# A row-sum kernel on one core: loads of contiguous 8 MB blocks, and sums stored block by block from ScalarE's queue

## The chip, the cores and the metric

The kernel runs on one NeuronCore of a Trainium2 chip. The metric is device time in microseconds (us); lower is better. Runs of one kernel on one chip agree to about 0.3%, so differences of 0.1 to 0.2% need several rounds, and most statements below about such differences rest on five. In the profiles DVE is VectorE, ACT is ScalarE, SP is SyncE; "SPq" and "ACTq" are the queues from which these two issue transfers. A transfer is carried out by 16 DMA engines as a list of descriptors, each of which moves one contiguous piece.

## The reference

```python
# x: (32, 512, 1024) float32
def reference(x):
    return np.sum(x, axis=-1).astype(np.float32)
```

The input is 16384 rows of 4 KB, 64 MB (67.1 million bytes) in all; the output is one float per row, 64 KB. Every byte is read once and added once, so this is a streaming problem.

## The kernel before

Partition `p` of 128 owns rows `128*p` to `128*p+127`. A tile is 16 rows of every partition (8 MB), three tiles are buffered, and VectorE and ScalarE sum eight rows each. One load is thus 128 pieces of 64 KB that lie 512 KB apart in memory. The last of the eight tiles is loaded in ever smaller pieces, so that little work is left after the last landing. One store of 64 KB ends the kernel.

```python
    C = R // P                                   # 128 rows per partition
    x_p = x_flat.rearrange("(p c) d -> p (c d)", p=P)
    out2d = out.rearrange("a (b c) -> (a b) c", c=C)
    G = 16                                       # rows per partition in a tile
    T = C // G                                   # 8 tiles
    xpool = ctx.enter_context(tc.tile_pool(name="x", bufs=3))
    ...
    def load(xt, c0, a, b):
        nc.sync.dma_start(out=xt[:, a:b], in_=x_p[:, c0 * D + a : c0 * D + b])
    ...
    for t in range(T - 1):
        c0 = t * G
        xt = xpool.tile([P, G * D], F32, tag="xt", name="xt")
        load(xt, c0, 0, G * D)
        rows_dve(xt, c0, 0, G // 2)              # one reduction of 8 rows
        rows_act(xt, c0, G // 2, G // 2)         # eight activations with a sum
    ...                                          # last tile: pieces of 8, 4, 2, 1 rows, then
    cuts = [j * D + k for k in (0, D // 2, 3 * D // 4, D)]      # the last row in three pieces
    ...
    acc = [part[:, 0:1], part[:, 1:2], res[:, C - 1 : C]]
    for i, (a, b) in enumerate(zip(cuts, cuts[1:])):
        pairs_dve(xt, a, b, acc[i - 1] if i else 0.0, acc[i])   # each step starts from the sum before
    nc.sync.dma_start(out=out2d, in_=res)
```

Of the kernel before, what the change touches and what calls it, by code (L numbers as in the profile page):

```python
# [1 line left out]

# [4 lines left out]

F32 = mybir.dt.float32
ADD = mybir.AluOpType.add


@with_exitstack
def kernel(
    ctx: ExitStack,
    tc: tile.TileContext,
    x: bass.AP,
    out: bass.AP,
):
    nc = tc.nc
    P = nc.NUM_PARTITIONS  # L20

    x_flat = x.flatten_outer_dims()
    R, D = x_flat.shape
    assert R % P == 0
    C = R // P

    x_p = x_flat.rearrange("(p c) d -> p (c d)", p=P)
    out2d = out.rearrange("a (b c) -> (a b) c", c=C)

    G = 16  # L30
    assert C % G == 0
    T = C // G

    xpool = ctx.enter_context(tc.tile_pool(name="x", bufs=3))
    rpool = ctx.enter_context(tc.tile_pool(name="res", bufs=1))
    res = rpool.tile([P, C], F32, name="res")
    part = rpool.tile([P, 4], F32, name="part")

    def load(xt, c0, a, b):
        nc.sync.dma_start(out=xt[:, a:b], in_=x_p[:, c0 * D + a : c0 * D + b])  # L40

    def rows_dve(xt, c0, j, n):
        nc.vector.tensor_reduce(  # L43
            out=res[:, c0 + j : c0 + j + n],
            in_=xt[:, j * D : (j + n) * D].rearrange("p (j d) -> p j d", d=D),
            axis=mybir.AxisListType.X,
            op=ADD,
        )

    def rows_act(xt, c0, j, n):  # L50
        for i in range(j, j + n):
            v = xt[:, i * D : (i + 1) * D]
            nc.scalar.activation(  # L53
                out=v,
                in_=v,
                func=mybir.ActivationFunctionType.Copy,
                accum_out=res[:, c0 + i : c0 + i + 1],
            )

    def pairs_dve(xt, a, b, first, acc):  # L60
        h = (b - a) // 2
        nc.vector.tensor_tensor_reduce(  # L62
            out=xt[:, a : a + h],
            in0=xt[:, a : a + h],
            in1=xt[:, a + h : b],
            scale=1.0,
            scalar=first,
            op0=ADD,
            op1=ADD,
            accum_out=acc,  # L70
# [5 lines that stand above are left out]
        load(xt, c0, 0, G * D)  # L76
        rows_dve(xt, c0, 0, G // 2)
        rows_act(xt, c0, G // 2, G // 2)

    c0 = (T - 1) * G  # L80
    xt = xpool.tile([P, G * D], F32, tag="xt", name="xt")
    j = 0
    runs = []
    for n in (8, 4, 2, 1):
        load(xt, c0, j * D, (j + n) * D)
        runs.append((j, n))
        j += n
    cuts = [j * D + k for k in (0, D // 2, 3 * D // 4, D)]
    for a, b in zip(cuts, cuts[1:]):
        load(xt, c0, a, b)  # L90

    for j, n in runs:
        if n > 1:
            rows_dve(xt, c0, j, n // 2)
            rows_act(xt, c0, j + n // 2, n // 2)
        else:
            rows_act(xt, c0, j, 1)
    acc = [part[:, 0:1], part[:, 1:2], res[:, C - 1 : C]]
    for i, (a, b) in enumerate(zip(cuts, cuts[1:])):
        pairs_dve(xt, a, b, acc[i - 1] if i else 0.0, acc[i])  # L100

    nc.sync.dma_start(out=out2d, in_=res)


# [1 line left out]
_INS = ['x']  # L106
_OUTS = [((32, 512), 'float32')]


# [23 lines left out]
```

## Time and profile before

| what | before |
|---|---|
| median of the runs | 163.95 us |
| span of the profiled run | 162.4 us |
| busy: DMA (loads' queue) / DVE / ACT | 96.3% / 43% / 43% |
| one 8 MB tile: load / DVE / ACT | 19.3 to 19.7 us / 8.69 us / 8.4 us |

From the page of the kernel before: busy time of two engines, the moved GB/s in 40 equal slices of the span, the DMA queues (packets, MB, share of 16 engines), and the chain of work that ended last (followed back from the last instruction, at each step to what released it), by engine and by line.

```profile
DVE 69.9 (43%) x16; ACT 69.0 (43%) x129; POOL 0.2 (0%) x4
...
GB/s 258 517 323 452 517 355 420 517 371 404 501 355 436 517 371 404 517 371 404 517 452 325 517 468 307 517 468 323 501 484 323 484 484 307 452 420 408 418 350 20
...
q1 hardware_dynamic: 2160, 67.18, 96.3%
...
DMA 85%; DVE 11%; SPq 1%; issue 1%; DVEq 0%
```

The loads fill the span and the two computing engines are idle more than half of it. A single slice above 500 GB/s is only the way in which whole 64 KB descriptors are booked into 4 us slices; the mean (414 GB/s over the span) is what counts.

From the timeline of DVE before: start, duration, instruction, and in brackets the idle time ahead of it and what ended it. One line is one tile's reduction, so the difference of two starts is the time of one load. The last line is the first step on the last row.

```profile
22.97 8.69 DVE L43 TENSOR_REDUCE res<-xt 128x8 f32<-128x8192 f32 x1 [22.97 <-DMA xt<-in_x_dram]
42.27 8.69 DVE L43 TENSOR_REDUCE res<-xt 128x8 f32<-128x8192 f32 x1 [10.62 <-DMA xt<-in_x_dram]
61.96 8.69 DVE L43 TENSOR_REDUCE res<-xt 128x8 f32<-128x8192 f32 x1 [11.00 <-DMA xt<-in_x_dram]
...
139.44 8.69 DVE L43 TENSOR_REDUCE res<-xt 128x8 f32<-128x8192 f32 x1 [10.66 <-DMA xt<-in_x_dram]
...
158.64 0.42 DVE L62 CUSTOM_DVE_ANT_0 xt<-xt 128x256 f32<-128x256 f32 x1 [0.87 <-DMA xt<-in_x_dram]
```

Each reduction waits some 10.7 us for its load. From the waits of SP's queue (who waited for whom: total us, times, longest) and the transfers of the page (size, us from issue to landing):

```profile
SPq L40 <- DVE res L43: 105.8, 5, 29.6
SPq L102 <- DVE res L62: 39.5, 1, 39.5
SPq L40 <- DMA xt<-in_x_dram: 7.8, 1, 7.8
...
out_dram<-res SPq DMA_DIRECT2D x1, 64.0 KB, 1.5
```

SP waits for buffers to come free, with a full queue of loads ahead; the one store lands in 1.5 us. The trace also records every DMA descriptor. A 64 KB one takes 2418 ns in nearly all cases, and 16 of them at a time give 16 x 65536 B / 2.418 us = 434 GB/s.

### The profile page before, as it was taken

The numbers are of one execution on the slowest core, as the hardware profiler recorded it, in microseconds if no ns is written. First come the engines' busy times: TensorE is split into PE (matmuls) and PEld (weight loads), VectorE is DVE, ScalarE is ACT, GpSimd is POOL, SyncE is SP. The second block draws the span as 40 slices with busy tenths as digits, with TensorE's granted clock in tenths as the row PEclk, the third lists the DMA queues.
The fourth block names the chain that finished last, engine by engine and source line by source line (L and its number), as shares of the span: only waits on it lengthen the run. The fifth ranks groups of instructions, "written<-read, shape, count | busy, mean of one in ns | idle before, by whom it ended". The sixth has DMA issues, their size and how long they took to land.

```text
span 162.4 us, 220 instructions
## 1 busy us (share of the span) xinstructions
DVE 69.9 (43%) x16; ACT 69.0 (43%) x129; POOL 0.2 (0%) x4
## 2 busy tenths in 40 slices
DVE  0000039700595007940099101990049700697882
ACT  3000039700594007930099101990039600696881
POOL 0000000000000000000000000000000000000000
DMA  7979989989989989989997997997997997999980
GB/s 258 517 323 452 517 355 420 517 371 404 501 355 436 517 371 404 517 371 404 517 452 325 517 468 307 517 468 323 501 484 323 484 484 307 452 420 408 418 350 20
DMA packets 2161, 67.18 MB, mean 414 GB/s; under 512 B 240, under 2 KB 624, under 8 KB 880
## 3 DMA queue, kind: packets, MB, share of 16 engines
q1 hardware_dynamic: 2160, 67.18, 96.3%
q14 instruction: 1, 0.01, 0.0%
HBM read 67.11 MB, written 0.07 MB: 414 GB/s over the span
## 4 chain that ended last, share of the span: by engine, by line
DMA 85%; DVE 11%; SPq 1%; issue 1%; DVEq 0%
DMA xt<-in_x_dram 85%; DVE res L43 11%; SPq L40 1%; DVE xt L62 0%; DVE part L62 0%; DVEq L62 0%; DVEq L128 0%
## 5 line engine op out<-in xcount | busy, mean ns | idle before, releaser
L43 DVE TENSOR_REDUCE res<-xt 128x8 f32<-128x8192 f32 (+3 forms) x10 | 68.7, 6873 | 89.0 <-DMA xt<-in_x_dram 89.0
L53 ACT ACTIVATE xt<-xt 128x1024 f32<-128x1024 f32 x64 | 66.7, 1043 | 89.3 <-DMA xt<-in_x_dram 89.1
L53 ACT ACTIVATION_READ_ACCUMULATOR xt<-xt 128x1 f32 x64 | 11.9, 187 | 0.0
L53 ACT ACT_TABLE_LOAD x1 | 1.3, 1283 | 0.7 <-PEq L117 0.7
L62 DVE CUSTOM_DVE_ANT_0 xt<-xt 128x256 f32<-128x256 f32 x1 | 0.4, 425 | 0.9 <-DMA xt<-in_x_dram 0.9
L62 DVE CUSTOM_DVE_ANT_0 xt<-xt,part 128x128 f32<-128x128 f32 x2 | 0.7, 352 | 0.1
L62 DVE DVE_READ_ACCUMULATOR2_ANT part<- 128x1 f32 x2 | 0.2, 82 | 0.0
L117 POOL MEMSET const-bfloat16-1.0<- 128x1 bf16 x1 | 0.1, 101 | 0.0
L117 POOL MEMSET const-uint8-127<- 128x1 uint8 x1 | 0.1, 101 | 0.0
L117 POOL MEMSET const-float32-0.0<- 128x1 f32 x1 | 0.1, 98 | 0.2 <-issue 0.2
L117 POOL MEMSET const-float32-1.0<- 128x1 f32 x1 | 0.1, 98 | 0.0
L62 DVE DVE_READ_ACCUMULATOR2_ANT res<- 128x1 f32 x1 | 0.1, 84 | 0.0
## 6 DMA issues: line engine op xcount, KB each, us to landing
xt<-in_x_dram SPq DMA_DIRECT2D x1, 4096.0 KB, 39.7
xt<-in_x_dram SPq DMA_DIRECT2D x1, 2048.0 KB, 44.2
xt<-in_x_dram SPq DMA_DIRECT2D x1, 1024.0 KB, 46.2
xt<-in_x_dram SPq DMA_DIRECT2D x1, 512.0 KB, 47.0
xt<-in_x_dram SPq DMA_DIRECT2D x1, 256.0 KB, 47.1
xt<-in_x_dram SPq DMA_DIRECT2D x2, 128.0 KB, 43.0
xt<-in_x_dram SPq DMA_DIRECT2D x7, 49.4
out_dram<-res SPq DMA_DIRECT2D x1, 64.0 KB, 1.5
```

What stands on the lines that cost most here:

```text
L40: nc.sync.dma_start(out=xt[:, a:b], in_=x_p[:, c0 * D + a : c0 * D + b])
L43: nc.vector.tensor_reduce(out=res[:, c0 + j : c0 + j + n], in_=xt[:, j * D : (j + n) * D].rearrange("p (j d) -> p j d", d=D), axis=mybir.A ...
L53: nc.scalar.activation(out=v, in_=v, func=mybir.ActivationFunctionType.Copy, accum_out=res[:, c0 + i : c0 + i + 1],)
L62: nc.vector.tensor_tensor_reduce(out=xt[:, a : a + h], in0=xt[:, a : a + h], in1=xt[:, a + h : b], scale=1.0, scalar=first, op0=ADD, op1=A ...
L117: nc = _bacc.Bacc("TRN2", target_bir_lowering=False, num_devices=1)
```

## The change

The intent: let each load read one contiguous 8 MB block, so that memory is walked in order, and send each block's 2048 sums away as soon as they are there. ScalarE's queue carries the stores, so that they need not stand in line behind the loads' issues on SP.

```diff
-    x_p = x_flat.rearrange("(p c) d -> p (c d)", p=P)
-    out2d = out.rearrange("a (b c) -> (a b) c", c=C)
-
     G = 16
     assert C % G == 0
     T = C // G
+    x_t = x_flat.rearrange("(t p j) d -> t p (j d)", p=P, j=G)
+    out_t = out.rearrange("a (b j) -> (a b) j", j=G).rearrange("(t p) j -> t p j", p=P)
...
-        nc.sync.dma_start(out=xt[:, a:b], in_=x_p[:, c0 * D + a : c0 * D + b])
+        nc.sync.dma_start(out=xt[:, a:b], in_=x_t[c0 // G, :, a:b])
...
         rows_act(xt, c0, G // 2, G // 2)
+        nc.scalar.dma_start(out=out_t[t], in_=res[:, c0 : c0 + G])
...
-    nc.sync.dma_start(out=out2d, in_=res)
+    nc.sync.dma_start(out=out_t[T - 1], in_=res[:, c0 : c0 + G])
```

The loads keep their number, size and descriptors (128 of 64 KB). The one store of 128 pieces of 512 B becomes eight stores of 128 pieces of 64 B.

## The prediction

> **What bounds the kernel now.** The load stream. The page gives DMA 96.3% of 16 engines' span for the one queue, DVE 43%, ACT 43%; the chain of waits is 85% "DMA xt<-in_x_dram". In the timeline the first reductions of successive tiles start at 22.97, 42.27, 61.96 ... 139.44 us: 19.30 to 19.69 us per tile, while a tile costs DVE 8.69 us and ACT about 8.4 us. Each load is 128 descriptors of 64 KB, eight per DMA engine; the DMA records nearly all show 2.42 us, so 16 x 65536 B / 2.42 us = 433 GB/s. The Trainium skill, "DMA: Bandwidth & Descriptors", section "Where 436 GB/s comes from", puts the ceiling of the SBUF ports at 435 GB/s; this trace agrees (433). So the memory side does not limit the old layout (one 64 KB piece every 512 KB), although the same page, section "Latency and other measured facts", warns of row pitches at large powers of two. This trace shows no loss at 512 KiB except about 0.5 us per engine in the first eight descriptors (first ones 2.5 to 3.4 us instead of 2.42) and about 0.3 us in the third tile.
>
> **What the change does.**
> 1. Loads: same count, descriptors and bytes; 8 MB contiguous instead of 128 pieces 512 KB apart. They are at the ports' pace already, so I expect 2.42 us again. At best the start-up and third-tile losses vanish: 0 to -0.8 us. If the new pitch (64 KB between partitions) hit the memory worse, descriptors over 2.5 us would show it; I give that about 5%.
> 2. Adds seven stores of 8 KB: 128 descriptors of 64 B each, eight per engine per store, on ScalarE's queue but on the same 16 DMA engines. A 512 B descriptor of the old final store takes 27 ns. Estimate for 64 B: 10 to 30 ns, so 0.1 to 0.25 us per store and engine, 0.6 to 1.7 us for seven if they displace load time fully; half of it hidden: +0.5 us.
> 3. ScalarE's issue of a store waits for VectorE (0.3 us), in an idle stretch of 10.7 us per tile: off the critical path.
> 4. Final store: 8 KB in 64 B pieces instead of 64 KB in 512 B pieces. Eight descriptors per engine of 27 ns are 0.2 us; at most -0.1 us, or +0.3 us if small writes are slow.
> 5. Stores take every other DMA semaphore, so the second-last small load waits for the seventh tile's landing (139.5 us). It is needed at about 158 us: no cost.
>
> **On the critical path:** the small stores' DMA time and the final store: about +0.4 us.
>
> **Predicted:** 164.4 us, range 163.4 to 166.2. Faster by over 2%: 1%; within 2%: 94%; slower by over 2%: 5%.
>
> **What the profile would show.** Right: load descriptors' median 2.42 us; tile intervals 19.3 to 19.7 us; a second DMA queue with under 1.5% of the engines' time; DVE and ACT busy near 70 us; chain over 80% loads; final store 1.4 to 1.9 us to landing. Wrong: tile intervals at 19.9 or more (stores dear, or the memory side), load descriptors clearly off 2.42 us, or a wait in the last tile for a piece issued late.
>
> **What would make it wrong.** Contiguous blocks colliding in memory; 64 B writes costing engines 100 ns or more each (7 x 8 x 100 ns = 5.6 us); a second queue's own start-up or drain; two queues breaking the overlap of successive 64 KB descriptors.

## The result

The changed kernel took 163.76 us (163.64 to 163.77, 4 runs) against 163.95 us (163.81 to 164.09, 4 runs). The ratio is 0.9987 with a 95% interval of 0.997 to 1.0004. Here and below a ratio is the mean time of one kernel's runs over that of the other's in the same rounds, so it is not quite the ratio of the medians. The result is correct.

The same lines of the page after. The second queue (q10) carries the early stores.

```profile
DVE 69.9 (43%) x16; ACT 69.0 (43%) x129; POOL 0.2 (0%) x4
...
q1 hardware_dynamic: 2160, 67.12, 96.4%
q10 hardware_dynamic: 1008, 0.06, 0.4%
...
DMA 86%; DVE 8%; ACT 3%; issue 1%; SPq 0%; DVEq 0%
DMA xt<-in_x_dram 72%; DMA out_dram<-res 14%; DVE res L42 7%; ACT xt L52 3%; DVE xt L61 0%; SPq L39 0%; DVE part L61 0%; DVEq L61 0%; DVEq L128 0%
```

The busy times are the same. New is that 14% of the chain goes through a store. That share is not a cost: the chain leads from a late load back to the store that held up its issue (109.12 to 131.84 us), but that load then lay in the queue behind others and landed at 158.17 us. The timeline of DVE after, the same tiles and the last row:

```profile
22.87 8.69 DVE L42 TENSOR_REDUCE res<-xt 128x8 f32<-128x8192 f32 x1 [22.87 <-DMA xt<-in_x_dram]
42.22 8.69 DVE L42 TENSOR_REDUCE res<-xt 128x8 f32<-128x8192 f32 x1 [10.67 <-DMA xt<-in_x_dram]
61.59 8.69 DVE L42 TENSOR_REDUCE res<-xt 128x8 f32<-128x8192 f32 x1 [10.69 <-DMA xt<-in_x_dram]
...
139.12 8.69 DVE L42 TENSOR_REDUCE res<-xt 128x8 f32<-128x8192 f32 x1 [10.69 <-DMA xt<-in_x_dram]
...
158.35 0.43 DVE L61 CUSTOM_DVE_ANT_0 xt<-xt 128x256 f32<-128x256 f32 x1 [0.89 <-DMA xt<-in_x_dram]
```

The tiles come every 19.35 to 19.40 us, and the seventh is 0.32 us earlier than before: 0.10 us of that is there at the first tile, the rest comes at the third, where the kernel before had some descriptors of up to 2893 ns. The waits of SP's queue and the stores of the page:

```profile
SPq L39 <- DVE res L42: 105.5, 5, 29.5
SPq L39 <- DMA out_dram<-res: 20.0, 3, 11.8
...
out_dram<-res ACTq DMA_DIRECT2D x7, 8.0 KB, 22.6
out_dram<-res SPq DMA_DIRECT2D x1, 8.0 KB, 1.4
```

This is the surprise of an otherwise uneventful result. A store of 8 KB takes 1.4 us when the loads are over, and 22.6 us beside them; and three of the last small loads waited for such stores, 20.0 us in all. They wait because the program uses eight DMA semaphores (counters by which transfers report that they have landed) in turn, and a transfer may reuse one only after its last user has landed. The last load was issued at about 145.5 us, where before it had been issued at 120.4 us. It still landed in time (VectorE starts on the last row at 158.35 us, against 158.64 us before; the last lines of the two timelines), so no time was lost. But it was closer than the small size of the stores suggests.

The trace's descriptor records show what a store does in these 22.6 us. The start of every sixteenth descriptor (one per DMA engine and row), in us, of the changed kernel's loads and of its first store, issued at 31.65 us:

```
64 KB load descriptors: 36.12 38.55 40.98       43.40 45.82 48.24 50.66 53.08
64 B store descriptors: 36.12 38.54 40.96 41.27 43.39 45.82 48.24 50.66
```

The store advances by one descriptor per engine for each load descriptor, with one extra at 41.27 us, where one load ends with its own small completion descriptor and the next begins. That suggests that a DMA engine serves its two queues in turn, one descriptor each. Another 4.5 us of the 22.6 pass between the store's issue and its first descriptor, against 0.8 us for the store at the end; why is not shown. The rival reading is that writing to memory is slow while reads run at full rate. Experiments 7 to 9 decide between these; experiments 1 to 6 ask where the 0.2 us came from.

### The profile page after: what moved, and what is told of

The parts are those of the page before. It is cut to its first block, busy times and chain, and to the rows that moved or that the text cites. A ratio compares the mean times of both kernels' runs of the same rounds, so it can differ in the third digit from the quotient of the medians.

```text
span 162.0 us, 229 instructions
## 1 busy us (share of the span) xinstructions
DVE 69.9 (43%) x16; ACT 69.0 (43%) x129; POOL 0.2 (0%) x4
## 4 chain that ended last, share of the span: by engine, by line
DMA 86%; DVE 8%; ACT 3%; issue 1%; SPq 0%; DVEq 0%
DMA xt<-in_x_dram 72%; DMA out_dram<-res 14%; DVE res L42 7%; ACT xt L52 3%; DVE xt L61 0%; SPq L39 0%; DVE part L61 0%; DVEq L61 0%; DVEq L128 0%
## 6 DMA issues: line engine op xcount, KB each, us to landing
out_dram<-res ACTq DMA_DIRECT2D x7, 8.0 KB, 22.6
```

## The experiments

### 1 to 4: one half of the change at a time, and both kernels again

These four ran on one chip in the same five rounds. Theory A says that contiguous loads gain and that small stores cost nearly as much; B, that neither matters beyond 0.2 us; C, that only the smaller final store gains.

New loads, old store (the outputs come in the wrong order):

```diff
 # against the changed kernel
-    out_t = out.rearrange("a (b j) -> (a b) j", j=G).rearrange("(t p) j -> t p j", p=P)
+    out2d = out.rearrange("a (b c) -> (a b) c", c=C)
...
-        nc.scalar.dma_start(out=out_t[t], in_=res[:, c0 : c0 + G])
...
-    nc.sync.dma_start(out=out_t[T - 1], in_=res[:, c0 : c0 + G])
+    nc.sync.dma_start(out=out2d, in_=res)
```

> New load layout alone, with the one 64 KB store of before (outputs in the wrong order on purpose, so a wrong result is right here). Theory A (two small effects of opposite sign: the small stores cost what was predicted, and contiguous loads pay for them): 0.5 to 0.9 us faster than before, since the stores' +0.3 to +0.6 us are gone. Rival B (neither part matters beyond 0.2 us): within 0.2 us of the changed kernel, that is -0.3 to 0 us against before. Rival C (the layout does nothing at all and the gain is the smaller final store): same as before within 0.1 us.

Old loads, new stores:

```diff
 # against the kernel before
+        nc.scalar.dma_start(out=out2d[:, c0 : c0 + G], in_=res[:, c0 : c0 + G])
...
-    nc.sync.dma_start(out=out2d, in_=res)
+    nc.sync.dma_start(out=out2d[:, c0 : c0 + G], in_=res[:, c0 : c0 + G])
```

> Old load layout with the new stores (seven of 64 B pieces on ScalarE's queue, the last from SP); result right. Theory A: 0.3 to 0.6 us slower than before. Rival B: within 0.15 us of before. Rival C: 0.1 to 0.2 us faster than before. All theories: each early store takes about 22 us from issue to landing, as in the changed kernel, and its second queue's descriptors 11 ns each.

The kernel before and the changed kernel, both without an edit:

> The kernel before, unchanged, as a control. Ratio 1.000 within 0.001. Its profile tells whether the slow descriptors at the start of the third tile (up to 2.89 us, tile interval 19.69 us in the first profile) belong to the old layout (they come back at 41 us) or are chance (absent, or elsewhere). If chance, the tile starts should end up 0.3 us earlier, near those of the changed kernel.

> The changed kernel, unchanged, timed in the same rounds as the other three. Ratio 0.998 to 0.9995 as in the first result; if it comes out at 1.000 the first difference was chance. Its profile tells whether the even tile intervals of 19.35 to 19.40 us repeat.

Measured:

| kernel | median us | ratio to before (95%) | first tile's sum starts | seventh tile's sum starts |
|---|---|---|---|---|
| 1 new loads, old store | 163.76 | 0.9976 (0.9964 to 0.9989) | 22.65 | 138.95 |
| 2 old loads, new stores | 164.12 | 1.0001 (0.9988 to 1.0013) | 23.07 | 139.45 |
| 3 before | 164.06 | 0.9994 (0.9981 to 1.0008) | 22.98 | 139.44 |
| 4 changed | 163.87 | 0.9983 (0.997 to 0.9995) | 22.74 | 139.22 |

The median of before over all nine of its runs here is 164.09 us. The small gain is in the loads (about 0.3 us), and the stores cost 0.06 us (2 against 3) to 0.11 us (4 against 1), which is less than the intervals of about 0.2 us to either side resolve. That is B for the stores, and a little more than B for the loads; C falls, because kernel 2 has the small final store too and gains nothing. The slow descriptors of the third tile were chance in their place: the control has a third tile of 19.56 us, kernel 2, with the same layout, one of 19.36 us. But the control's seventh tile did not come 0.3 us earlier, as expected for chance: it is at 139.44 us again, because other tiles lost time. Nor did the even intervals of the changed kernel repeat: kernel 4 has a fourth tile of 19.66 us. From the first to the seventh sum the changed kernel takes 116.25 us in its first profile and 116.48 us in kernel 4, against 116.47 and 116.46 us with before (first profile and 3). So kernel 4 has its whole lead over the control at the first tile, while in the first two profiles only 0.10 of 0.32 us were there.

The records show what the seven stores do to an engine. The descriptors carry no engine number, so I chained them by time (each starts where one ended). A 64 B descriptor takes 11 ns. In kernels 1 and 3 an engine's successive load descriptors overlap by some 3 to 4 ns, in kernels 2 and 4 they stand about 3 ns apart: summed over the 56 large ones, -0.15 us becomes +0.17 us, a cost of 0.32 us per engine. The time of the load descriptors themselves, summed per engine, differs from profile to profile by more than that, with stores (136.08 to 136.40 us over the first profile of the changed kernel, 2, 4, 10 and 11) as without (136.20 to 136.64 us over the first profile of before, 1, 3, 5 and 6). So these records do not tell why the 0.32 us do not show up in the time.

### 5 and 6: is the loads' gain at the start?

In the profiles at hand, 15 of the 16 engines had begun their first descriptor by 2.70 to 2.84 us in the old layout (before, 2, 3) and by 2.04 to 2.16 us in the new one (after, 1, 4). Profiles taken later were less clear-cut in this (2.08 to 2.59 us with a contiguous first load). Either only the first tile matters, or all do.

```diff
 # 5, against the kernel before (6 has "c0 > 0"); sums wrong on purpose
+    x_t = x_flat.rearrange("(t p j) d -> t p (j d)", p=P, j=G)
...
-        nc.sync.dma_start(out=xt[:, a:b], in_=x_p[:, c0 * D + a : c0 * D + b])
+        src = x_t[c0 // G, :, a:b] if c0 == 0 else x_p[:, c0 * D + a : c0 * D + b]
+        nc.sync.dma_start(out=xt[:, a:b], in_=src)
```

> The kernel before, with only the first tile's load taken from a contiguous 8 MB block (sums wrong on purpose). Theory A (the new layout gains at the start only: the 16 DMA engines begin their first descriptors closer together): the first reduction starts at 22.6 to 22.9 us instead of 22.97 to 23.07, most engines start by 2.1 us, and the time is 0.2 to 0.4 us under before. Rival B (the gain is spread over the run, fewer slow descriptors in every tile): first reduction near 23.0 us, or time within 0.1 us of before.

> The reverse: the first tile as before, all others from contiguous blocks (sums wrong on purpose). Theory A: first reduction at about 23.0 us, time within 0.1 us of before. Rival B: 0.2 to 0.4 us under before.

Measured: 5 took 164.00 us (ratio 0.9995, 0.9982 to 1.0009), 6 took 163.85 us (0.9988, 0.9976 to 1.0001), before 164.06 us. The first sums started at 22.73 us in 5 and at 23.05 us in 6. So the first half of theory A holds: a contiguous first load lands 0.1 to 0.6 us earlier, in every profile that was taken (sums start at 22.46 to 22.87 us in the eight with such a load in one piece, at 22.97 to 23.07 us in the four with the old one). The second half failed: in 5 the start was gained and the time was not. By the times alone both came out as rival B said: 5 within 0.1 us of before, 6 0.2 us under it without the better start. But the intervals of about 0.2 us to either side do not separate the two theories. The timeline of DVE in kernel 5 shows where the gain went in the one profiled run (164.13 us; the other four, 163.86 to 164.14 us, have no profile):

```profile
80.75 8.69 DVE L45 TENSOR_REDUCE res<-xt 128x8 f32<-128x8192 f32 x1 [10.67 <-DMA xt<-in_x_dram]
100.74 8.69 DVE L45 TENSOR_REDUCE res<-xt 128x8 f32<-128x8192 f32 x1 [11.31 <-DMA xt<-in_x_dram]
```

This tile took 19.99 us. At 85.09 us the records hold an 8 KB transfer of the instruction queue (q14), 309 ns long, and just then one engine's chain has a gap of 302 ns and a load descriptor of 2785 ns, some 0.7 us lost by that one engine. A load lands when its slowest engine is done: this engine ends the seventh tile at 138.97 us, the next slowest at 138.38 us. Every profile has one such transfer within the span, between 70 and 88 us. Whether it costs anything depends on whether the engine that it falls on is a late one. So the sizes add up poorly at this scale, and I do not claim to know where in the run the whole 0.2 to 0.3 us of the new layout arises.

### 7: shorter load descriptors

If a store waits for one load descriptor per descriptor of its own, shorter load descriptors make it land sooner.

```diff
 # against the changed kernel
-        load(xt, c0, 0, G * D)
+        for h in range(4):
+            load(xt, c0, h * 4 * D, (h + 1) * 4 * D)
```

> The changed kernel with each of the seven 8 MB loads split into four loads of 16 KB per partition. Theory A (a DMA engine takes one store descriptor after each load descriptor, so a store's eight descriptors last eight load descriptors): the store's descriptors come 0.61 us apart on an engine and the store lands after 6 to 8 us instead of 22.6. Rival B (the 22 us are the latency of writing memory beside full-rate reads): still about 22 us. Both: the loads cost four times 611 ns instead of 2418 ns, so about 26 ns more per 64 KB, 1.5 us in all: 165.2 us, 0.9% slower than before.

The store's line of the transfers:

```profile
out_dram<-res ACTq DMA_DIRECT2D x7, 8.0 KB, 9.1
```

It lands in 9.1 us instead of 22.6 us, though the stores are the same and memory is read about as fast (411 against 415 GB/s over the span). That is longer than the 6 to 8 us that I expected, but far from 22, and the store's eight rows of descriptors take 4.1 to 4.7 us from first to last instead of 15.4 us. Much of the rest is time before the first descriptor: the first store is issued at 26.87 us and starts at 30.46 us. The rival falls. The time was 165.42 us (ratio 1.008, 1.0066 to 1.0094): four descriptors of 611 ns in place of one of 2418 ns cost 26 ns more, times 56 per engine 1.5 us, as expected.

### 8: more store descriptors than load descriptors

In the changed kernel a store has eight data descriptors and a completion descriptor per engine, and so has a load. The stores just keep up. Two stores per tile have twice as many.

```diff
 # against the changed kernel
-        nc.scalar.dma_start(out=out_t[t], in_=res[:, c0 : c0 + G])
+        for h in (0, G // 2):
+            nc.scalar.dma_start(out=out_t[t, :, h : h + G // 2], in_=res[:, c0 + h : c0 + h + G // 2])
```

> The changed kernel with each of the seven early stores cut in two (32 B pieces, one for VectorE's half, one for ScalarE's), so sixteen store descriptors per engine and tile against eight load descriptors. Theory A (one store descriptor per load descriptor): the store ring cannot keep up, the stores fall behind by 19 us per tile, land up to 60 us and more after their issue, and the seventh load, whose semaphore was last used by the third tile's first store, is issued only when the load queue has run dry near 120 us: a gap in the loads of 3 to 4 us, in all 2 to 5% slower (167 to 172 us). Rival B (latency only): every store lands in about 23 us, no gap, time within 0.5% of the changed kernel.

It took 166.67 us (ratio 1.0158, 1.0144 to 1.0172): slower by 2.6 us than before, for the same bytes. That is just under the 167 to 172 us that I had expected, with a gap of the expected kind, though of 2.3 us instead of 3 to 4. The timeline of DVE, the waits of SP's queue, and the landings of the stores (shortest, median, longest) in this kernel:

```profile
119.66 8.69 DVE L42 TENSOR_REDUCE res<-xt 128x8 f32<-128x8192 f32 x1 [10.70 <-DMA xt<-in_x_dram]
141.74 8.69 DVE L42 TENSOR_REDUCE res<-xt 128x8 f32<-128x8192 f32 x1 [13.40 <-DMA xt<-in_x_dram]
```

```profile
SPq L39 <- DMA out_dram<-res: 81.4, 5, 31.5
```

```profile
DMA to landing us min/median/max: 1.4/25.4/61.3
```

The seventh tile takes 22.08 us instead of 19.4. The records, by start of the first and of the last data descriptor of each store in us, show why:

```
stores 1 to 5:   36.2-51.5  55.5-70.8  74.9-90.2  94.3-109.6  113.7-118.8
stores 6 to 10:  118.8-118.9  118.9-118.9  118.9-119.0  119.0-119.2  119.2-119.6
load descriptors (every sixteenth): 113.71 116.13 120.90 123.92 126.34
```

One store takes a whole tile's time while loads run, and two are added per tile, so they fall behind. The seventh load waits for the semaphore of the fifth store (the first half of the third tile's), issued at 70 us and landed only at 119.8 us. By then the loads that were queued ahead have run out. With nothing to take turns with, five more stores drain in under 1 us. The load is issued at 119.93 us and starts at 120.90 us, 2.3 us later than the pace asks, and its first descriptors are slow as at the start of the kernel (3.02 us to the next row). So the slow landing of a small store is not harmless in itself: it costs as soon as something that the loads need hangs on it.

### 9: the stores on the loads' own queue

```diff
 # against the changed kernel
-        nc.scalar.dma_start(out=out_t[t], in_=res[:, c0 : c0 + G])
+        nc.sync.dma_start(out=out_t[t], in_=res[:, c0 : c0 + G])
```

> The changed kernel with the seven early stores issued from SP, so that they share the loads' queue (the scheduler then issues the load of tile t+2 only after the store of tile t; one load is still queued ahead, so no gap is expected). Theory A (two queues take turns descriptor by descriptor, one queue goes in order): the store's eight descriptors follow the one load queued ahead back to back: issue to landing 11 to 13 us instead of 22.6, and on one engine they come about 0.01 us apart instead of 2.42. Rival B (latency of memory writes beside reads): landing still 22 us or more. Time within 0.2 us of the changed kernel under both.

The store's line, two lines of DVE's timeline at the end of this kernel, and the line of the changed kernel that matches the second:

```profile
out_dram<-res SPq DMA_DIRECT2D x8, 8.0 KB, 10.8
```

```profile
148.79 4.42 DVE L42 TENSOR_REDUCE res<-xt 128x4 f32<-128x4096 f32 x1 [1.07 <-DMA xt<-in_x_dram]
155.60 2.29 DVE L42 TENSOR_REDUCE res<-xt 128x2 f32<-128x2048 f32 x1 [2.39 <-DMA xt<-in_x_dram]
```

```profile
153.75 2.29 DVE L42 TENSOR_REDUCE res<-xt 128x2 f32<-128x2048 f32 x1 [0.52 <-DMA xt<-in_x_dram]
```

The landing took 10.8 us, and all 128 data descriptors of a store begin within 0.7 us (for instance 41.05 to 41.71), right after the load ahead of them. One queue goes in order; two take turns. The expectation for the time was wrong: 166.10 us (ratio 1.0118, 1.0101 to 1.0134). I had overlooked the last tile. Its second piece is issued by SP behind the seventh tile's store, which waits for that tile's sums until 147.8 us, while the only load queued ahead ends near 148.8 us. The queue runs dry, and the reduction of that piece waits 2.39 us instead of 0.5 us. This is what ScalarE's queue spares the change.

### 10 and 11: a shorter tail

In no run did a 64 KB load descriptor take less than 2.42 us, so what is left to try is the end: three chained VectorE steps after the last landings.

```diff
 # 10, against the changed kernel; 11 is the changed kernel without an edit
-    cuts = [j * D + k for k in (0, D // 2, 3 * D // 4, D)]
+    cuts = [j * D + k for k in (0, D // 2, D)]
...
-    acc = [part[:, 0:1], part[:, 1:2], res[:, C - 1 : C]]
+    acc = [part[:, 0:1], res[:, C - 1 : C]]
```

> The changed kernel with the last row cut in two pieces of 512 columns instead of 512, 256 and 256: one chained VectorE step fewer after the last landing (0.35 us plus 0.08 us), against a step that is 0.07 us longer (0.42 for 0.35 us). If the last piece has landed by 158.9 us, VectorE ends about 0.2 us earlier: 163.55 to 163.75 us against 163.76 to 163.87 of the changed kernel. If the landing is what it waits for, no gain.

> The changed kernel in the same rounds as the two above, as their base. Ratio to before again 0.998 to 0.999.

Kernel 10 took 163.69 us (0.9979, 0.9964 to 0.9993), kernel 11, the changed one, 163.83 us (0.9984, 0.9972 to 0.9996), before 164.10 us. From the first of these last steps to the end of the last, DVE takes 1.07 us in 10 (158.44 to 159.51) and 1.22 us in 11 (158.21 to 159.43). That is 0.15 us less, although VectorE ends 0.08 us later in the profile of 10, whose last row came later. The medians differ by 0.14 us, but the intervals overlap, so this is a likely gain of 0.1%, not a shown one. It is the fastest correct version, and no version was faster than before by more than 0.3%.

## Why the prediction was right

The time lay inside the range (163.76 us against 163.4 to 166.2 us), and "within 2%" was the likely one. The middle of the range was on the wrong side, though: +0.4 us was predicted and -0.2 us measured. The reason for "no change" was the right one: the loads ran at 2.42 us per descriptor in both layouts, 434 GB/s, which agrees with the 435 GB/s ceiling of the SBUF ports that the Trainium skill gives ("DMA: Bandwidth & Descriptors", "Where 436 GB/s comes from"). The nicer order in memory did not raise this rate. That the ports set it is the page's account, and the figures agree; no run here separates the ports from another limit of the same size. Point by point:

1. **Loads, 0 to -0.8 us.** Inside the range: about -0.3 us (experiment 1), though the predicted sum counted nothing for it. The reason is open. The start-up loss that the prediction named, slow first descriptors, did not shrink: over the first eight it is 0.55 to 0.74 us per engine in before, 2 and 3, and 0.64 to 0.78 us in the first profile of the changed kernel, 1 and 4. What came earlier with the contiguous load is the start itself: the 16 engines start at 2.14 to 2.25 us on average in the former three, at 1.85 to 1.93 us in the latter. Experiment 6 gained 0.2 us without that, inside the noise. The third tile's loss was chance in its place.
2. **Early stores, +0.5 us.** The mechanism was right and the size was off. A 64 B descriptor takes 11 ns, inside the 10 to 30 ns of the estimate, and 56 of them are 0.62 us per engine. Half of this showed up between load descriptors (0.32 us), as written. But the time grew by only 0.06 to 0.11 us. So of the 0.6 us between the predicted +0.4 us and the measured -0.2 us, about half lies in this term and half in the loads.
3. **ScalarE's wait for VectorE off the critical path.** Right: ACT still sits idle for 10.9 us before a tile (10.93 us before the one at 100.36 us, and 10.97 us before the same tile in the kernel before), waiting for its load.
4. **Final store.** Right: 1.4 us to landing instead of 1.5 us.
5. **Semaphores, no cost.** Right in the result, incomplete in the reason. The prediction named only the seventh load as what a late piece would wait for. One piece does wait for it (issued at 139.11 us), but three others wait for stores. The prediction did not mention these waits, and never asked how long a small store takes beside a full load queue. It takes 22.6 us, and the last piece was issued at 145.5 us because of it. That this cost nothing was thus partly luck: experiment 8 shows the same mechanism costing 2.6 us. It is also why one sign foreseen for the profile failed, "chain over 80% loads": the loads have 72% of the chain and a store 14%.

The two queues did disturb the back-to-back run of load descriptors, as the list of dangers said, by about 7 ns each.

## What to carry to other kernels

When the descriptors of a stream already run at the pace of the ports (here 2.42 us per 64 KB on each engine), a change of the order in memory has little to gain: here 0.3 us of 164, for a reason that stays open. Look at descriptor durations before planning a layout. A small transfer on a second queue took little of the engines' time here (11 ns per 64 B descriptor), but it advances by one descriptor per descriptor of the big stream: compare the counts per engine (8 against 8 kept up, 16 against 8 did not), and keep anything that the loads wait for, here a recycled semaphore, off its landing. Placing it in the loads' own queue made it land sooner (10.8 us), but SP issues in order, and so the next load had to wait for the sums.

## What the Trainium skill lacked or had wrong

- "DMA: Bandwidth & Descriptors", section "Queues, rings and completion order", says that an engine goes round its queues at packet granularity, with 9 to 17 descriptors to a typical packet. In these runs it changed queues after every single 64 KB load descriptor, and after every single 64 B store descriptor as long as loads were waiting: store descriptors came 2.42 us apart. The page does not say what follows for a small transfer beside large ones: 22.6 us to landing instead of 1.4 us, and 9.1 us with 16 KB load descriptors.
- The same page, section "Issuing engines are not separate DMA queues", says that issuing from several engines only saves the sequencer's time. Here the choice of queue changed the landing of the same store from 22.6 us (ScalarE's queue) to 10.8 us (SP's), and, because SP issues in order, the total from 163.83 to 166.10 us.
- The same page, section "Specifications", has a read-modify-write below 512 B. The engine time does not show one: 64 B write descriptors took 11 ns, 512 B ones 27 ns. What happens in memory is not shown.
- The same page, section "Latency and other measured facts", warns of row pitches at large powers of two. Its figures are for copies between tensors in memory; for loads alone, a pitch of 512 KiB left the typical descriptor at 2.42 us (434 GB/s), as with 64 KB, and the whole kernel 0.3 us of 164 slower (experiment 1). The first tile landed 0.1 to 0.6 us later.
- "Runtime: NRT & Kernel Launch", section "Instruction fetch mechanics", calls the cost of a fetch mostly hidden. For the issuing engine that may be so. In a kernel bound by DMA one 8 KB fetch took some 0.7 us from one DMA engine, and in the profile of experiment 5 this was the engine that the tile waited for.
